# Block sums, bonus sums and transposes of an RWKV-7 inverse issued one step later than the vector operations that they read

## The chip, the cores and the metric

The kernel runs on one core of a Trainium2 chip. Its five engines each work through their own instructions in order: TensorE (PE in the profile; PEld is its weight load), VectorE (DVE), ScalarE (ACT), GpSimd (POOL) and SyncE (SP). An instruction that waits for another engine holds up everything behind it on its own. The metric is the device time of one execution in microseconds; less is better.

## The reference

Three transformer blocks follow one another on 512 tokens of width 1024. Only the second matters here: a normalised input is projected, a part of the columns goes through an RWKV-7 recurrence of six heads of 64, a part through block attention ("moba"), a part through a gated MLP; the three are joined, projected and followed by a feed-forward part. The recurrence, cut to what the change touches:

```
kk = heads(k * k_k)
kk = kk / jnp.maximum(jnp.linalg.norm(kk, axis=-1, keepdims=True), 1e-12)
k = k * (1.0 + (a - 1.0) * k_a)
...
def step(state, inp):
    r_t, w_t, k_t, v_t, kk_t, a_t = inp
    sa = jnp.einsum('bhij,bhj->bhi', state, -kk_t)
    state = (state * w_t[:, :, None, :]
             + sa[..., :, None] * (kk_t * a_t)[:, :, None, :]
             + v_t[..., :, None] * k_t[:, :, None, :])
    return state, jnp.einsum('bhij,bhj->bhi', state, r_t)
...
_, y = lax.scan(step, s0, xs)
...
bonus = jnp.sum(rh * kh * r_k.astype(jnp.float32), axis=-1, keepdims=True) * vh
out = (y + bonus.reshape(B, S, D_RWKV)) * g.astype(jnp.float32)
```

## The kernel before

The 512 recurrence steps are not run one by one. Six heads make three pairs (0, 1, 2), since two heads of 64 fill 128 partitions, and the tokens are cut in chunks of 64. Inside a chunk the steps become a triangular system, so each pair has three generators:

- `rw_e(p)` prepares: gates, exponentials and products of the inputs, and the bonus. VectorE makes t1 = r * r_k * k (line 1598), TensorE sums it over each head with a matrix of ones (`bon`, line 494 as all matmuls of the helper `mm`), VectorE multiplies the sum by v (line 1605). GpSimd makes two products, `b * kk` (line 1595) and `be` (line 1630; its tile shows as aa); VectorE's `ke` follows it (line 1631).
- `rw_solve(p)` inverts the triangular matrices. It makes the scores `sc` (masked on VectorE, line 1657), takes their diagonal 16 by 16 blocks, and spreads them over free columns in four products `mv` (line 1678; two on VectorE, two on GpSimd, 480, 352, 224 and 96 columns). TensorE sums each within blocks (`ab`), ScalarE copies the sum back (line 1683). Fifteen steps of two VectorE instructions (`tm`, `tc`, lines 1690 and 1692) give the inverse of the small blocks; it is spread into two matrices T (line 1695, one half on VectorE, one on GpSimd), transposed on TensorE (`Tn`, line 1700), and two levels of products (`inv`, `invT`, `invN`) with predicated copies (lines 1722 and 1723) extend it to 64 by 64.
- `rw_chain(p)` uses the inverse: `nat` transposes and their copies RW (lines 1844 to 1849), `akv`, W (copied on VectorE, line 1878), Rt, Y and the matrices M (masked to MN on VectorE, line 1900). Then the state goes through eight chunks: S on TensorE, st on VectorE (line 1914), one after the other.

What sets the order of instructions is a list of such Python generators that are stepped in turn. Each `yield` names a number of nanoseconds, and `run` always steps the generator whose sum of yields is smallest. These numbers are a schedule on paper, not times. Three calls of `run` hold the work of this part, each beside a share of the attention (`mo`, the moba generator: `at` scores, their softmax on VectorE and ScalarE with the exponentials `prob`, `pT` transposes, `ao`):

```
run(par.rest(), mo.part(MOP[0]))
run(slow(CS, rw_chain(0)), rw_solve(1), rw_e(2), mo.part(MOP[1]))
run(slow(CS, rw_chain(1)), rw_solve(2), mo.part(MOP[2]), rw_end(0))
```

The names used below: **stage A** is the end of the projections (`pj`) with `rw_solve(0)` and `rw_e(1)`, up to 1632 us in the profile; **stage B** is the second of these lines, to 1702 us; **stage C** the third, to 1762 us. `lg`, `mean`, `hs` and `hb` belong to `rw_end`, the normalisation and gate of a finished pair. All matmul results take one of 8 PSUM banks.

Of the kernel before, what the change touches and what calls it, by code (L numbers as in the profile page):

```python
# [16 lines left out]
OP = mybir.AluOpType  # L17
# [297 lines left out]
def kernel(ctx: ExitStack, tc: tile.TileContext, A, out):  # L315
    nc = tc.nc
    V, P, SC, PE = nc.vector, nc.gpsimd, nc.scalar, nc.tensor
# [7 lines left out]
    def T(name, dt=F32, n=512):  # L325
        return heap.tile([128, n], dt, name=name, tag="t")
# [4 lines left out]
    def SM(name, n, dt=F32):  # L331
        assert n <= 32
        return glob.tile([128, n], dt, name=name, tag="sm", bufs=24)

    def PS(name="ps"):
        return psum.tile([128, 512], F32, name=name, tag="ps")
# [6 lines left out]
    def vec(n, i=0, w=1):  # L343
        o, _ = _VOFF[n]
        return vecs[:, o + i:o + i + w]

    def con(n, i=0, w=None):
        o, ww = _COFF[n]
        w = ww if w is None else w
        return cons[:, o + i:o + i + w]  # L350
# [13 lines left out]
    def tok(t):  # L364
        return slice(128 * t, 128 * t + 128)
# [127 lines left out]
    def mm(ps, a, b, start, stop, **kw):  # L493
        PE.matmul(ps, a, b, start=start, stop=stop, **kw)  # L494
# [82 lines left out]
    def nosync(a, b):  # L577
        tc.add_manual_dep(a.ins, b.ins.name,
                          mybir.DependencyInfo(mybir.DependencyClass.NoSync, mybir.DependencyReason.DATA),
                          reason="table")  # L580
# [9 lines left out]
    def act(out_, in_, func, **kw):  # L590
        o = SC.activation(out_, in_, func, **kw)
        nosync(o, phase["mark"])
        phase["ops"].append(o)
# [157 lines left out]
    for k in range(KD):  # L751
# [4 lines left out]
        h, l = hx(k)  # L756
# [101 lines left out]
    for o in range(0, _NM, 512):  # L858
        a = T("mf")
        w = min(512, _NM - o)  # L860
# [446 lines left out]
    for e in range(NE):  # L1307
# [29 lines left out]
        for q in range(8):  # L1337
            w, rel = ws.raw()
            for kk in range(2):
                f = 2 * q + kk  # L1340
                p, c, j = f // 8, (f // 4) % 2, f % 4
# [239 lines left out]
    bon = {}  # L1581
    el = {}

    def rw_e(p):

        rT, kT, vT = ya.pop(p), ya.pop(3 + p), ya.pop(6 + p)
        kkn, b, l = kk.pop(p), aa.pop(p), lw.pop(p)
        cum = T("cum")
        V.tensor_tensor_scan(cum, r64, l, 0.0, op0=OP.mult, op1=OP.add)
        yield 800  # L1590

        t1 = T("t1")
        V.tensor_scalar(t1, b, -1.0, vec("rwkv_k_a_2", p), op0=OP.add, op1=OP.mult)
        V.scalar_tensor_tensor(kT, t1, 1.0, kT, op0=OP.add, op1=OP.mult)
        P.tensor_tensor(b, b, kkn, op=OP.mult)
        yield 1200

        V.scalar_tensor_tensor(t1, rT, vec("rwkv_r_k_2", p), kT, op0=OP.mult, op1=OP.mult)
        pb = PS("bon")
        mm(pb, con("blk64"), t1, True, True)  # L1600
        at = l
        V.tensor_tensor(at, cum, l, op=OP.subtract)
        yield 1500
        bon[p] = t1
        V.tensor_tensor(t1, pb, vT, op=OP.mult)
        c8 = cum.rearrange("p (n c) -> p n c", c=64)
        ke = T("ke")
        V.tensor_tensor(ke.rearrange("p (n c) -> p n c", c=64), c8[:, :, 63:64].to_broadcast([128, 8, 64]), c8,
                        op=OP.subtract)
        yield 1500  # L1610
        pc = SM("pc", 8)
        act(pc, c8[:, :, 63], AF.Exp)
        ei = T("ei")
        act(ei, cum, AF.Exp, scale=-1.0)
        act(at, at, AF.Exp)
        yield 1400
        act(cum, cum, AF.Exp)
        act(ke, ke, AF.Exp)
        V.scalar_tensor_tensor(at, kkn, -1.0, at, op0=OP.mult, op1=OP.mult)
        yield 1300  # L1620
        bh = kkn
        V.tensor_tensor(bh, b, ei, op=OP.mult)
        yield 800
        V.tensor_tensor(cum, cum, rT, op=OP.mult)
        yield 800
        kh = ei
        V.tensor_tensor(kh, kT, ei, op=OP.mult)
        yield 800
        be = b
        P.tensor_tensor(be, b, ke, op=OP.mult)  # L1630
        V.tensor_tensor(ke, kT, ke, op=OP.mult)
        yield 1400
        el[p] = at, cum, bh, kh, be, ke, vT, pc

# [2 lines left out]
    def rw_solve(p):  # L1637
# [10 lines left out]
        for t in range(TT):  # L1648
# [6 lines left out]
            for h in range(2):  # L1655
                a = sb[h][:, 512 * t:512 * t + 512]
                V.tensor_tensor(a.rearrange("p (x s) -> p x s", x=2), pss[h].rearrange("p (x s) -> p x s", x=2), m4,
                                op=OP.mult)
# [11 lines left out]
        i32, i16 = c32.rearrange("p (x i) -> p x i", x=8), c16.rearrange("p (x i) -> p x i", x=8)  # L1670
        V.tensor_scalar(i16, i32[:, :, :16], con("half32", 0, 1), None, op0=OP.mult)
        V.scalar_tensor_tensor(i16, i32[:, :, 16:], con("half32", 1, 1), i16, op0=OP.mult, op1=OP.add)

        ab = []
        for g in range(4):
            w = 15 - 4 * g
            mv = T("mv")
            (P if g % 2 else V).tensor_tensor(mv[:, :32 * w].rearrange("p (j x i) -> p j x i", j=4, x=8),
                               i16[:, None, :, 4 * g + 1:].to_broadcast([128, 4, 8, w]),
                               con("eye16", 4 * g, 4)[:, :, None, None].to_broadcast([128, 4, 8, w]), op=OP.mult)  # L1680
            ps = PS("ab")
            mm(ps[:, :32 * w], con("blk16"), mv[:, :32 * w], True, True)
            SC.copy(mv[:, :32 * w], ps[:, :32 * w])
            ab.append(mv[:, :32 * w].rearrange("p (j x i) -> p j x i", j=4, x=8))
            yield 700
        t16, m16 = tc.rearrange("p (x i) -> p x i", x=8), tm.rearrange("p (x i) -> p x i", x=8)
        P.tensor_copy(t16, con("eye16")[:, None, :].to_broadcast([128, 8, 16]))
        for j in range(15):
            w = 15 - j
            V.tensor_tensor(m16[:, :, :w], ab[j // 4][:, j % 4, :, j % 4:], t16[:, :, j:j + 1].to_broadcast([128, 8, w]),  # L1690
                            op=OP.mult)
            V.tensor_tensor(t16[:, :, j + 1:], t16[:, :, j + 1:], m16[:, :, :w], op=OP.add)
            yield 500
        for h in range(2):
            (P if h else V).tensor_tensor(
                Tt[h].rearrange("p (x b i) -> p x b i", x=4, b=8), t16[:, 4 * h:4 * h + 4, None, :].to_broadcast([128, 4, 8, 16]),
                con("own16")[:, None, :, None].to_broadcast([128, 4, 8, 16]), op=OP.mult)
            pa = PS("Tn")
            for t in range(TT):
                PE.transpose(pa[:, tok(t)], Tt[h][:, tok(t)], ident)  # L1700
            SC.copy(Tn[h], pa)
            yield 800
# [34 lines left out]
    def e0():  # L1737
        while "exp" not in flag:
            yield 1000
        yield from rw_e(0)  # L1740
        yield from bundle(rw_solve(0), wait(5000, rw_e(1)))
# [205 lines left out]
    mo = Persist(moba())  # L1947
# [3 lines that stand above are left out]
    m2 = lambda k, s=slice(0, 512): (m2p[k][0][:, s], m2p[k][1][:, s])  # L1951

# [513 lines left out]
```

## Time and profile before

| what | value |
|---|---|
| three runs, median (lowest to highest) | 3088.91 us (3085.46 to 3089.7) |
| the profiled execution | 3089.25 us |
| its span, first to last instruction | 3087.5 us |
| mean granted TensorE clock over the span | 0.973 |
| busy over the span: TensorE, VectorE, ScalarE, GpSimd | 92%, 41%, 26%, 15% |
| the three stages | 1590 to 1762 us of the span |

The shares of busy time are means over the whole program, most of which is large matrix products with TensorE full. The part that is changed covers some 172 of 3087.5 us and has to be read by itself. Times in the rows are microseconds from the span's start; a bracket after an instruction gives the idle time of its engine just before it and the instruction that ended that. A row with x4 stands for four instructions back to back. The granted clock is that of TensorE as a share of full speed.

### The profile page before, as it was taken

The numbers are of one execution on the slowest core, as the hardware profiler recorded it, in microseconds if no ns is written. First come the engines' busy times: TensorE is split into PE (matmuls) and PEld (weight loads), VectorE is DVE, ScalarE is ACT, GpSimd is POOL, SyncE is SP. The second block draws the span as 40 slices with busy tenths as digits, with TensorE's granted clock in tenths as the row PEclk, the third lists the DMA queues.
The fourth block names the chain that finished last, engine by engine and source line by source line (L and its number), as shares of the span: only waits on it lengthen the run. The fifth ranks groups of instructions, "written<-read, shape, count | busy, mean of one in ns | idle before, by whom it ended". The sixth has DMA issues, their size and how long they took to land.

```text
span 3087.5 us, 34890 instructions
## 1 busy us (share of the span) xinstructions
PE 2825.3 (92%) x13860; PEld 1847.5 (60%) x13860; DVE 1278.5 (41%) x2361; ACT 788.3 (26%) x1629; POOL 472.6 (15%) x440
## 2 busy tenths in 40 slices
PE   7989979998888888887997899999998989999999
PEld 4866564442222222224875678888886756788887
DVE  4157551112112111114376663333699753453334
ACT  3233220100000000004232332323343343442322
POOL 2035230000000000002220111001154332310100
PEclk8999979999999999998998999999999999999999
DMA  6123538999999999995110122323322212422221
GB/s 261 69 82 130 219 142 329 389 421 422 421 421 421 421 421 421 421 420 227 68 42 1 56 99 93 116 70 107 109 103 90 84 47 92 160 83 103 109 87 64
DMA packets 99011, 605.28 MB, mean 196 GB/s; under 512 B 11008, under 2 KB 11136, under 8 KB 31008
## 3 DMA queue, kind: packets, MB, share of 16 engines
q1 hardware_dynamic: 98640, 602.39, 49.6%
q8 instruction: 109, 1.79, 0.2%
q0 software_dynamic: 208, 0.66, 0.1%
q14 instruction: 54, 0.44, 0.0%
HBM read 592.52 MB, written 10.49 MB: 195 GB/s over the span
## 4 chain that ended last, share of the span: by engine, by line
PE 60%; DMA 24%; DVE 10%; ACT 2%; issue 2%; POOL 2%; SPq 0%; DVEq 0%; POOLq 0%; ACTq 0%
PE pj L494 25%; PE pn L494 15%; DMA wb<-in_w_up_dram 9%; DMA w<-in_w_up_dram 5%; DMA w<-in_w_down_dram 4%; PE pg L494 4%; DMA wb<-in_w_down_dram 4%; DVE cv L2146 2%; PE py L494 2%; PE at L494 2%; PE sp L494 1%; PE xs L494 1%; PE pc L494 1%; PE ao L494 1%; PE kv L494 1%
## 5 line engine op out<-in xcount | busy, mean ns | idle before, releaser
L443 DVE TENSOR_TENSOR wl<-w,wh 128x512 fp32r<-128x512 f32 (+1 forms) x422 | 299.0, 752 | 204.3 <-ACT wh L442 156.1
L494 PE MATMUL pg<-wb,xs 128*64 128x512 f32 x1184 | 284.7, 609 | 38.2 <-DMA wb<-in_w_up_dram 21.2
L442 ACT CAST wh<-w 128x512 fp32r<-128x512 f32 (+1 forms) x516 | 292.0, 617 | 99.1 <-PE pn L494 92.3
L494 PE MATMUL pg<-w,xs 128*64 128x512 f32 x824 | 197.0, 602 | 27.8 <-DMA w<-in_w_up_dram 15.0
L572 POOL TENSOR_TENSOR r<-m,mhalf 128x1 f32<-128x1 f32 x46 | 31.1, 678 | 1206.5 <-DVE m L618 1201.0
L494 PEld LDWEIGHTS pg<-wb,xs 128*64 128x64 f32 x1184 | 76.9, 138 | 220.8 <-issue 127.9
L494 PE MATMUL pn<-wh,fh 128*128 128x512 f32 x432 | 168.1, 389 | 0.0
L494 PE MATMUL pn<-wh,fl 128*128 128x512 f32 x432 | 168.1, 389 | 0.0
L494 PE MATMUL pn<-wl,fh 128*128 128x512 f32 x432 | 168.1, 389 | 0.0
L2146 DVE SCALAR_TENSOR_TENSOR cv<-glua,vecs,cv 128x507 f32<-128x507 f32 (+27 forms) x232 | 164.4, 735 | 4.2
L494 PE MATMUL py<-wb,hidT 128*64 128x512 f32 x600 | 142.4, 601 | 25.3 <-DMA wb<-in_w_down_dram 25.3
L443 POOL TENSOR_TENSOR wl<-w,wh 128x512 fp32r<-128x512 f32 x94 | 125.2, 1351 | 150.4 <-ACT wh L442 135.6
L494 PEld LDWEIGHTS pg<-w,xs 128*64 128x64 f32 x824 | 52.4, 136 | 152.6 <-issue 84.5
L494 PE MATMUL pj<-h2fh,wh 128*128 128x512 f32 (+1 forms) x376 | 141.4, 378 | 2.5 <-ACT h2fh L644 2.5
L494 PE MATMUL pj<-h2fl,wh 128*128 128x512 f32 (+1 forms) x376 | 141.7, 377 | 0.0
L494 PE MATMUL pj<-h2fh,wl 128*128 128x512 f32 (+1 forms) x376 | 141.6, 377 | 0.0
L1335 DVE TENSOR_TENSOR sg<-sg,pg 128x512 f32<-128x512 f32 x16 | 11.0, 688 | 292.1 <-PE pg L494 292.1
L494 PE MATMUL pj<-h3h,wh 128*128 128x512 f32 (+1 forms) x336 | 128.4, 382 | 0.6 <-ACT h3h L644 0.6
L494 PE MATMUL pj<-h3l,wh 128*128 128x512 f32 (+1 forms) x336 | 125.5, 373 | 0.6 <-DVE h3l L646 0.6
L494 PE MATMUL pj<-h3h,wl 128*128 128x512 f32 (+1 forms) x336 | 125.6, 374 | 0.0
L1352 DVE SCALAR_TENSOR_TENSOR yg<-py,gsl,g2h 128x512 f32<-128x512 f32 x16 | 12.0, 751 | 269.7 <-PE py L494 269.7
L494 PE MATMUL py<-w,hidT 128*64 128x512 f32 x424 | 102.4, 606 | 19.9 <-DMA w<-in_w_down_dram 19.9
(615 smaller groups left out, 5682.3 us busy)
## 6 DMA issues: line engine op xcount, KB each, us to landing
wb<-in_w_gate_dram SPq DMA_DIRECT2D x75, 1024.0 KB, 19.8
wb<-in_w_down_dram SPq DMA_DIRECT2D x75, 1024.0 KB, 19.8
wb<-in_w_up_dram SPq DMA_DIRECT2D x73, 1024.0 KB, 19.8
w<-in_w_down_dram SPq DMA_DIRECT2D x53, 1024.0 KB, 19.8
w<-in_w_up_dram SPq DMA_DIRECT2D x52, 1024.0 KB, 19.8
w<-in_w_gate_dram SPq DMA_DIRECT2D x51, 1024.0 KB, 19.8
w<-in_w_in_dram SPq DMA_DIRECT2D x35, 1024.0 KB, 4.9
w<-in_w_ff_dram SPq DMA_DIRECT2D x30, 1024.0 KB, 4.8
```

The costliest lines, as they stand in the source:

```text
L442: SC.copy(hi, src)
L443: (eng or V).tensor_tensor(lo, src, hi.bitcast(F32), op=OP.subtract)
L494: PE.matmul(ps, a, b, start=start, stop=stop, **kw)
L572: P.tensor_tensor(y, m, mhalf[:, :n], op=OP.pow)
L1335: V.tensor_tensor(sg, sg, pu, op=OP.mult)
L1352: V.scalar_tensor_tensor(a, py, gsl[:, e:e + 1], g2h, op0=OP.mult, op1=OP.mult)
L2146: V.scalar_tensor_tensor(acc[:, sh:], a[:, :512 - sh], w[j], acc[:, sh:], op0=OP.mult, op1=OP.add)
```

## The change

Three places are edited. In `rw_e` the bonus sum moves from right behind t1 to behind the exponentials, two yields later, and the product with v to the end. In `rw_solve` each block sum and its copy come one g later, behind the next product `mv`, with one more yield ahead of the last. And both T products come first, then a yield of 1500, then the transposes of both halves. The added yields are 700 + 1500 on paper for each pair.

```diff
--- before.py
+++ after.py
@@ -1596,13 +1596,9 @@
         yield 1200
 
         V.scalar_tensor_tensor(t1, rT, vec("rwkv_r_k_2", p), kT, op0=OP.mult, op1=OP.mult)
-        pb = PS("bon")
-        mm(pb, con("blk64"), t1, True, True)
         at = l
         V.tensor_tensor(at, cum, l, op=OP.subtract)
         yield 1500
-        bon[p] = t1
-        V.tensor_tensor(t1, pb, vT, op=OP.mult)
         c8 = cum.rearrange("p (n c) -> p n c", c=64)
         ke = T("ke")
         V.tensor_tensor(ke.rearrange("p (n c) -> p n c", c=64), c8[:, :, 63:64].to_broadcast([128, 8, 64]), c8,
@@ -1616,6 +1612,8 @@
         yield 1400
         act(cum, cum, AF.Exp)
         act(ke, ke, AF.Exp)
+        pb = PS("bon")
+        mm(pb, con("blk64"), t1, True, True)
         V.scalar_tensor_tensor(at, kkn, -1.0, at, op0=OP.mult, op1=OP.mult)
         yield 1300
         bh = kkn
@@ -1629,6 +1627,8 @@
         be = b
         P.tensor_tensor(be, b, ke, op=OP.mult)
         V.tensor_tensor(ke, kT, ke, op=OP.mult)
+        bon[p] = t1
+        V.tensor_tensor(t1, pb, vT, op=OP.mult)
         yield 1400
         el[p] = at, cum, bh, kh, be, ke, vT, pc
 
@@ -1671,18 +1671,27 @@
         V.tensor_scalar(i16, i32[:, :, :16], con("half32", 0, 1), None, op0=OP.mult)
         V.scalar_tensor_tensor(i16, i32[:, :, 16:], con("half32", 1, 1), i16, op0=OP.mult, op1=OP.add)
 
-        ab = []
-        for g in range(4):
-            w = 15 - 4 * g
-            mv = T("mv")
-            (P if g % 2 else V).tensor_tensor(mv[:, :32 * w].rearrange("p (j x i) -> p j x i", j=4, x=8),
-                               i16[:, None, :, 4 * g + 1:].to_broadcast([128, 4, 8, w]),
-                               con("eye16", 4 * g, 4)[:, :, None, None].to_broadcast([128, 4, 8, w]), op=OP.mult)
+        ab, mvs = [], []
+
+        def ab_sum(g):
+            w, mv = 15 - 4 * g, mvs[g]
             ps = PS("ab")
             mm(ps[:, :32 * w], con("blk16"), mv[:, :32 * w], True, True)
             SC.copy(mv[:, :32 * w], ps[:, :32 * w])
             ab.append(mv[:, :32 * w].rearrange("p (j x i) -> p j x i", j=4, x=8))
+
+        for g in range(4):
+            w = 15 - 4 * g
+            mv = T("mv")
+            mvs.append(mv)
+            (P if g % 2 else V).tensor_tensor(mv[:, :32 * w].rearrange("p (j x i) -> p j x i", j=4, x=8),
+                               i16[:, None, :, 4 * g + 1:].to_broadcast([128, 4, 8, w]),
+                               con("eye16", 4 * g, 4)[:, :, None, None].to_broadcast([128, 4, 8, w]), op=OP.mult)
             yield 700
+            if g:
+                ab_sum(g - 1)
+        yield 700
+        ab_sum(3)
         t16, m16 = tc.rearrange("p (x i) -> p x i", x=8), tm.rearrange("p (x i) -> p x i", x=8)
         P.tensor_copy(t16, con("eye16")[:, None, :].to_broadcast([128, 8, 16]))
         for j in range(15):
@@ -1695,6 +1704,8 @@
             (P if h else V).tensor_tensor(
                 Tt[h].rearrange("p (x b i) -> p x b i", x=4, b=8), t16[:, 4 * h:4 * h + 4, None, :].to_broadcast([128, 4, 8, 16]),
                 con("own16")[:, None, :, None].to_broadcast([128, 4, 8, 16]), op=OP.mult)
+        yield 1500
+        for h in range(2):
             pa = PS("Tn")
             for t in range(TT):
                 PE.transpose(pa[:, tok(t)], Tt[h][:, tok(t)], ident)
```

The number of instructions is the same on every engine, and the order of GpSimd and SyncE does not change. TensorE, VectorE and ScalarE differ from the first bonus sum (about 1568 us in the profile) to the last `invT` of pair 2 (1761 us); ahead of it and behind it all orders are the same.

TensorE in stage B, from the last `pT` of pair 0's attention step (bon is the bonus sum of pair 2, akv and nat are pair 0's chain). Before:

```order
L1791 MATMUL pT<-cons,prob 128x128 x3
L494 MATMUL bon<-t_9078,cons 128x512
L494 MATMUL akv<-RW,sc_8623 128x128
L494 MATMUL akv<-RW,sc_8624 128x128
L1844 MATMUL nat<-cons,lwd 128x128
L1844 MATMUL nat<-cons,aa 128x128
L1844 MATMUL nat<-cons,ke 128x128
L1844 MATMUL nat<-cons,ya_8013 128x128
L494 MATMUL ao<-probT,v_8466 64x512 x2
```

and now:

```order
L1802 MATMUL pT<-cons,prob 128x128 x3
L494 MATMUL akv<-RW,sc_8623 128x128
L494 MATMUL akv<-RW,sc_8624 128x128
L1855 MATMUL nat<-cons,lwd 128x128
L1855 MATMUL nat<-cons,aa 128x128
L1855 MATMUL nat<-cons,ke 128x128
L1855 MATMUL nat<-cons,ya_8013 128x128
L494 MATMUL ao<-probT,v_8466 64x512 x2
```

The bonus sum has left this place; it now stands 34 rows further down, behind the first M group and an ao. The first block sums of pair 1, with W, Y, akv, Rt and M of pair 0's chain, before:

```order
L494 MATMUL ab<-mv,cons 128x480
L494 MATMUL W<-RW,T 128x128 x2
L494 MATMUL ab<-mv,cons 128x352
L494 MATMUL at<-qk 128x128 x2
L494 MATMUL Y<-sc_8623,W 64x128
L494 MATMUL Y<-sc_8624,W 64x128
L494 MATMUL Y<-sc_8623,RW 64x128
L494 MATMUL Y<-sc_8624,RW 64x128
L494 MATMUL ab<-mv,cons 128x224
L494 MATMUL akv<-RW,sc_8623 128x128
L494 MATMUL akv<-RW,sc_8624 128x128
L494 MATMUL Rt<-sc_8623,W 64x128
```

and now:

```order
L494 MATMUL W<-RW,T 128x128 x2
L494 MATMUL at<-qk 128x128 x2
L494 MATMUL Y<-sc_8623,RW 64x128
L494 MATMUL Y<-sc_8624,RW 64x128
L494 MATMUL ab<-mv,cons 128x480
L494 MATMUL akv<-RW,sc_8623 128x128
L494 MATMUL akv<-RW,sc_8624 128x128
L494 MATMUL Rt<-sc_8623,W 64x128
L494 MATMUL Y<-sc_8623,W 64x128
L494 MATMUL Rt<-sc_8624,W 64x128
L494 MATMUL Y<-sc_8624,W 64x128
```

W, the at of 128 columns and a pair of Y now stand ahead of the first block sum (480 columns), and akv, Rt and Y directly behind it; the other three block sums come after the M group. The transposes of pair 1 in the same stage, with the state chain (S, Y) of pair 0, before:

```order
L494 MATMUL M<-RW,bkz 128x128
L494 MATMUL Y<-rt,MN 128x64
L1700 MATMUL Tn<-cons,T 128x128 x8
L494 MATMUL S<-MN 128x128
L494 MATMUL inv<-T,sc_9047 128x128 x4
L494 MATMUL inv<-T,sc_9048 128x128 x4
L494 MATMUL S<-st,MN 128x128
L494 MATMUL Y<-rt,st 128x64
L1791 MATMUL pT<-cons,prob 128x128 x8
```

and now:

```order
L494 MATMUL M<-RW,bkz 128x128
L494 MATMUL S<-MN 128x128
L494 MATMUL Y<-rt,MN 128x64
L1711 MATMUL Tn<-cons,T 128x128 x4
L494 MATMUL S<-st,MN 128x128
L494 MATMUL Y<-rt,st 128x64
L1802 MATMUL pT<-cons,prob 128x128 x4
L1711 MATMUL Tn<-cons,T 128x128 x4
L1802 MATMUL pT<-cons,prob 128x128 x4
L494 MATMUL inv<-T,sc_9047 128x128 x4
```

One S moves ahead of the transposes, another with its Y goes between their halves, and eight of the attention's pT now stand ahead of the first inv. In stage C the first block sum of pair 2 stood ahead of W, lg and the at of 512 columns, and now stands behind them.

## Rows read from the trace of the kernel before

**Rows 1.** Stretches: length, each engine's busy us, TensorE clock, DMA share, GB/s.
```profile
1590.00:1612.00 22.00, 18.72 (x67) 13.31 (x67) 18.59 (x48) 6.23 (x14) 8.40 (x10) 0.84 0.00 1
...
1632.00:1656.00 24.00, 14.85 (x104) 9.45 (x102) 15.72 (x31) 6.49 (x19) 4.43 (x7) 0.85 0.00 1
...
1656.00:1683.00 27.00, 18.98 (x112) 13.35 (x112) 20.23 (x90) 7.39 (x24) 2.06 (x4) 0.88 0.00 1
...
1683.00:1702.00 19.00, 18.95 (x144) 16.95 (x145) 6.97 (x16) 5.12 (x10) 0.81 (x1) 0.91 0.00 1
...
1718.00:1746.00 28.00, 22.48 (x136) 14.63 (x137) 22.24 (x74) 9.09 (x25) 4.22 (x5) 0.88 0.24 81
```

**Rows 2.** TensorE's waits from 1590 to 1770: total, times, longest.
```profile
PE ab L494 <- DVE mv L1678: 10.2, 3, 5.3
PE bon L494 <- DVE t L1598: 5.9, 2, 4.2
```

**Rows 3.** The chain of waits from 1635 to 1658: start, us, what.
```profile
1636.36 2.05 PE bon L494 x2
...
1651.29 1.72 POOL aa L1630
...
1656.34 1.94 PE ab L494 x2
```

**Rows 4.** TensorE, stage B: start, us, instruction, [idle before, and releaser].
```profile
1631.59 0.55 PE L1791 MATMUL pT<-cons,prob 128*128 128x128 f32 x3
1636.36 2.05 PE L494 MATMUL bon<-t,cons 128*128 128x512 f32 x2 [4.22 <-DVE t L1598]
1638.20 1.06 PE L494 MATMUL akv<-RW,sc 128*128 128x128 f32 x4
...
1656.34 1.94 PE L494 MATMUL ab<-mv,cons 128*128 128x480 f32 x2 [5.27 <-DVE mv L1678]
```

**Rows 5.** ScalarE, stage B, the copy that makes akv's operand.
```profile
1628.38 0.27 ACT L1849 COPY RW<-nat 128x128 f32<-128x128 f32 x1
```

**Rows 6.** VectorE, stage B.
```profile
1638.44 0.69 DVE L1605 TENSOR_TENSOR t<-bon,ya 128x512 f32<-128x512 f32 x1 [1.63 <-PE bon L494]
...
1643.18 1.29 DVE L1657 TENSOR_TENSOR sc<-sc,cons 128x512 f32<-128x512 f32 x2 [3.60 <-PE sc L494]
...
1655.54 0.66 DVE L1678 TENSOR_TENSOR mv<-c,cons 128x480 f32<-128x480 f32 x1
...
1659.17 0.42 DVE L1878 COPY W<-W 128x256 f32<-128x256 f32 x1 [2.98 <-PE W L494]
...
1682.21 0.69 DVE L1695 TENSOR_TENSOR T<-tc,cons 128x512 f32<-128x512 f32 x1
```

**Rows 7.** TensorE, stage A.
```profile
1593.02 1.12 PE L494 MATMUL bon<-t,cons 128*128 128x512 f32 x2 [1.67 <-DVE t L1598]
1595.39 3.86 PE L494 MATMUL ab<-mv,cons 128*128 128x480 f32 x6 [1.25 <-DVE mv L1678]
```

**Rows 8.** TensorE, stage C.
```profile
1721.95 1.94 PE L494 MATMUL ab<-mv,cons 128*128 128x480 f32 x2 [3.63 <-DVE mv L1678]
1723.68 1.06 PE L494 MATMUL W<-RW,T 128*128 128x128 f32 x4
```

**Rows 9.** VectorE, stage C.
```profile
1724.78 0.42 DVE L1878 COPY W<-W 128x256 f32<-128x256 f32 x1 [2.13 <-PE W L494]
...
1728.03 0.30 DVE L1758 TENSOR_TENSOR at<-at,cons 128x128 f32<-128x128 f32 x1 [0.79 <-PE at L494]
```

**Rows 10.** VectorE, the state chain, stage B.
```profile
1685.45 0.29 DVE L1914 TENSOR_TENSOR st<-S,MN 128x128 f32<-128x128 f32 x1 [2.55 <-PE S L494]
```

**Rows 11.** VectorE's line 1594 in A and B, and GpSimd beside the latter.
```profile
1591.49 0.69 DVE L1594 SCALAR_TENSOR_TENSOR ya<-t,ya 128x512 f32<-128x512 f32 x1
...
1632.85 1.50 DVE L1594 SCALAR_TENSOR_TENSOR ya<-t,ya 128x512 f32<-128x512 f32 x1
...
1632.55 1.26 POOL L1595 TENSOR_TENSOR aa<-aa,kk 128x512 f32<-128x512 f32 x1 [19.98 <-DVE t L1593]
```

## The prediction

> **What bounds the kernel now.** I started from the table of stretches [rows 1]. The five stretches shown are the ones whose instruction order changes, in stages A (1590 to 1612 us), B (1632 to 1702) and C (1718 to 1746). The reader is to see that no engine is full in four of them: TensorE works 14.85 of 24 us in the second, VectorE 15.72. TensorE's mean granted clock is 0.84 to 0.88 there, so part of each runs at the lower of its two levels (1.2 instead of 2.4 GHz). DMA is idle but for 0.24 in the last. So this part is bound by hand-overs between engines. Only 1683 to 1702 is full: TensorE 18.95 of 19.
>
> The waits of TensorE [rows 2] then name what ends last. Block sums wait 10.2 us for the `mv` products, bonus sums 5.9 us for t1. Both are operands that VectorE or GpSimd makes, and the consumer stands directly behind in program order. The chain of waits [rows 3] shows that these are on the path: it goes through the bonus sum at 1636.36, through GpSimd's `be` at 1651.29 and through the block sum at 1656.34. A microsecond taken off here should reach the end, since what follows is the same order of instructions on every engine and no transfer fills those stages.
>
> **The change, part by part.** Nothing is added or removed; the sum consists of waits.
>
> *The bonus sum (edit a), stage B.* The bonus sum of pair 2 stands at the head of TensorE's queue from the last pT (1631.59 + 0.55 = 1632.14) to 1636.36 and costs a wait of 4.22 us; it then takes 2.05 us [rows 4]. The same pair of matmuls took 1.12 us in stage A [rows 7], so after the wait the engine was at the lower clock. Behind it stood `akv`, whose operand ScalarE had finished by 1628.38 + 0.27 [rows 5]: it was ready and not served for nine microseconds. With the sum moved behind the first `M` group, `akv` can start at about 1632.2 instead of 1638.20, 6.0 us earlier. How much of that gets through VectorE decides. VectorE has two waits there that come from the late TensorE, 1.63 us for the bonus sum and 3.60 us for the scores [rows 6]; both go, 5.2 us. Its product with vT, 0.69 us [rows 6], also moves behind the solve's first `mv` product. So that product, at 1655.54 now, comes 5.2 + 0.7 = 5.9 us earlier. The bounds are 4 us (TensorE's wait alone) and 8.3 us (all idle time of VectorE in that stretch, 24 - 15.72 [rows 1]). I take 5.9, because both waits have their cause directly in the moved instruction; the later wait of `ke` for GpSimd's `be` stays.
>
> *The block sums (edit b), stage B.* Before, ab of 480 columns waits 5.27 us [rows 4] with W, the third `at` group and Y behind it, and VectorE's copy of W waits 2.98 us in consequence [rows 6]. Afterwards W, at and Y are ahead of it. The 2.98 us can go entirely, or not at all if VectorE only reaches the recurrence when the sum and its copy are ready; between 0 and 3.0 I take 2.1, nearer the row, since some of the block sum's own wait remains (about 2.5 us, with a shorter queue behind it). Some VectorE work that stood inside the fifteen steps now runs ahead of them, which shortens the steps by what it lengthens the start: nothing. T of stage B, at 1682.21 now [rows 6], so comes 5.9 + 2.1 = 8.0 us earlier, with bounds 4 and 10.
>
> *The transposes (edit c).* Both T products go out first, and pair 1's first transposes now stand behind one S and Y of the state chain. An S step's answer took VectorE a wait of 2.55 us [rows 10], so the loss is up to that. Against it, 1683 to 1702 ran at 0.91 [rows 1]: 9% of 19 us, 1.7 us, can come back. I take zero; bounds +2.5 and -1.7.
>
> *Stage A.* The bonus sum of pair 1 leaves the place ahead of the first block sum. Its wait of 1.67 us goes, but the block sum, which waited 1.25 us more [rows 7], needs the same `mv` product at the same time. The wait becomes one of about 4 us, and what stands behind it starts no earlier. Zero; bounds: a gain of 2 us (a transpose wait covered by `at` work) and a loss of 2 us (lower clock behind the longer wait; the block sums ran at it before too, six taking 3.86 us [rows 7]).
>
> *Stage C.* Here W, lg and the last `at` group pass the first block sum. TensorE had waited 3.63 us there and then ran W at the lower clock in 1.06 us [rows 8]; VectorE waited 2.13 us for W and 0.79 us for at [rows 9]. They fit into TensorE's wait, so 2.9 us of VectorE's waits go. The stretch's clock of 0.88 over 28 us [rows 1] holds another 3.4 us, of which I count a third, because other waits remain. Gain 4.0 us, bounds 2 (transposes now behind the last pT and ao work) and 6.3.
>
> Sum: 0 - 8.0 + 0 - 4.0 = -12.0 us. The profiled execution took 3089.25 us (span 3087.5 and 1.75 around it), 0.34 above the median of the three runs, so 3089.25 - 12 gives **3077 us**.
>
> **Where a rule speaks against it.** `be` of stage B is a GpSimd product of two SBUF operands, and the edit brings VectorE's two-operand work closer around it. Beside a GpSimd product of this kind, VectorE's 128x512 instruction at 1632.85 took 1.50 us, and 0.69 us where none ran [rows 11]. GpSimd's product ended at 1632.55 + 1.26 = 1633.81, and VectorE's 0.54 us later, nearly its whole own duration. The Trainium skill, page "SBUF — State Buffer", section "Who interferes with whom", says that a VectorE instruction with two SBUF inputs and a GpSimd instruction that reads SBUF exclude each other, the later one waiting to the end of the first. This pair of rows agrees with it.
>
> **The rivals.**
> 1. *The stall only moves.* If VectorE is the real bound of stages B and C (20.23 of 27 us from 1656 to 1683 [rows 1]), the first `mv` product gains little, and only TensorE's 4.22 us wait is saved: 3089.25 - 4 = 3085 us. For it: the 10.2 us of block-sum waits are waits for VectorE or GpSimd. Against it: VectorE itself waits for TensorE in the same stretches (3.60, 2.98, 2.13).
> 2. *Slower: the state chain gets in front of the transposes.* In stages B and C the transposes come behind S and Y, which wait for VectorE's st. One such hop is 2.55 us [rows 10]; two in B and one in C would be 7.6 us, and the time 3089.25 + 7.6 = 3097 us, if T came no earlier. It decides from the point where T gains less than these hops cost. Against it: in B the state chain starts before T is ready, so its first hop is hidden when T is the later one.
> 3. *Exclusion by GpSimd.* If in each of the three stages one further VectorE instruction is held as above, for 0.8 us (1.50 - 0.69) up to `be`'s 1.72 us [rows 3], 2.4 to 5.2 us are lost from the 12: 3080 to 3082 us. For it: the 1.50 us row. Against it: `be` itself keeps its place in GpSimd's order and VectorE's `ke` waits for it anyway.
>
> **How the numbers follow.** Forecast 0.60; the stall only moves 0.18; slower 0.08; exclusion 0.14. The likeliest ends at 3077. Its bounds are -4 - 2 + 2.5 + 2 = -1.5 us with every term at its worst end and -10 - 6.3 - 1.7 - 2 = -20 at its best, which will not all fall together; half of each distance gives 3073 to 3082. Rival 3 lies in that, rival 1 at 3085 above it. For eight in ten the range goes from 3070 to 3085.5, which takes in rival 1's centre and leaves out the slower one. Differences under 0.2% (6.2 us) can't be told from none: faster than 3082.7 has 0.60 + 0.14 = 0.74, same 0.18, slower 0.08.
>
> **What would show it.** Edit a is right if `akv` of stage B starts about 1632 and no bonus sum waits over 1 us. It is wrong if `akv` is early and the first `mv` product still comes after 1653. Edit b: the first block sum of B at about 1650 with a wait near 2.5 us, that of C with a wait under 1.5 us, and VectorE's waits of 2.98 and 2.13 us gone. In A the first block sum should wait about 4 us and still start near 1595.4. T of B should stand at about 1674, and that of C some 12 us earlier than now. Edit c is right if from T to pair 1's last invT takes no longer than now (1682 to 1702). The forecast falls if T of B comes less than 4 us earlier, if the transposes wait for S, or if a stage after 1762 gives the gain back.

## The result and the profile after

The changed kernel takes 3063.86 us (median of 4, 3061.51 to 3067.9), against 3087.2 us for the kernel before (4 runs beside it, 3085.46 to 3089.7): a ratio of 0.9924, 95% interval [0.9912, 0.9936]. That is faster, and by 23 us instead of the 12 us forecast; the time lies below the range of 3070 to 3085.5. Its profiled execution took 3067.9 us with a span of 3066.1.

The first and last instruction of each stage tell where the time went. The line numbers of these rows are 9 to 11 higher than before. From the timelines of both kernels: the first `mv` product of a stage and T on VectorE, and the first `nat` transpose behind the last invT on TensorE, which ends the stage. Before (the products and T of stage B are in [rows 6]):

```profile
1594.59 0.66 DVE L1678 TENSOR_TENSOR mv<-c,cons 128x480 f32<-128x480 f32 x1
...
1610.96 0.69 DVE L1695 TENSOR_TENSOR T<-tc,cons 128x512 f32<-128x512 f32 x1
...
1627.52 0.27 PE L1844 MATMUL nat<-cons,lwd 128*128 128x128 f32 x1
...
1701.86 0.27 PE L1844 MATMUL nat<-cons,lwd 128*128 128x128 f32 x1
...
1721.14 0.66 DVE L1678 TENSOR_TENSOR mv<-c,cons 128x480 f32<-128x480 f32 x1
...
1744.76 0.69 DVE L1695 TENSOR_TENSOR T<-tc,cons 128x512 f32<-128x512 f32 x1
...
1761.43 0.27 PE L1844 MATMUL nat<-cons,lwd 128*128 128x128 f32 x1
```

After:

```profile
1594.11 0.66 DVE L1687 TENSOR_TENSOR mv<-c,cons 128x480 f32<-128x480 f32 x1
...
1609.40 0.69 DVE L1704 TENSOR_TENSOR T<-tc,cons 128x512 f32<-128x512 f32 x1
...
1624.27 0.27 PE L1855 MATMUL nat<-cons,lwd 128*128 128x128 f32 x1
...
1645.51 0.64 DVE L1687 TENSOR_TENSOR mv<-c,cons 128x480 f32<-128x480 f32 x1
...
1667.34 0.69 DVE L1704 TENSOR_TENSOR T<-tc,cons 128x512 f32<-128x512 f32 x1
...
1686.24 0.27 PE L1855 MATMUL nat<-cons,lwd 128*128 128x128 f32 x1
...
1705.63 0.64 DVE L1687 TENSOR_TENSOR mv<-c,cons 128x480 f32<-128x480 f32 x1
...
1725.18 0.69 DVE L1704 TENSOR_TENSOR T<-tc,cons 128x512 f32<-128x512 f32 x1
...
1738.72 0.27 PE L1855 MATMUL nat<-cons,lwd 128*128 128x128 f32 x1
```

Differences of these starts give the stretch that the change can touch: 1761.43 - 1594.59 = 166.84 us before, 144.61 us after, 22.2 us less. The rest of the program gave nothing of it back: from the last row to the end of the span it is 1326.07 us before and 1327.38 after. I use this stretch as the measure in all that follows, because it starts up to 8 us apart between profiled executions of the kernels below, which blurs a single time but not the stretch. A stretch is still that of one execution: the last section shows 1.5 us between executions with the same order.

| part | before | after | forecast | measured |
|---|---|---|---|---|
| A, `mv` product to T | 16.37 | 15.29 | 0 | -1.1 |
| A, T to the end | 16.56 | 14.87 | 0 | -1.7 |
| B, start to the `mv` product | 28.02 | 21.24 | -5.9 | -6.8 |
| B, product to T | 26.67 | 21.83 | -2.1 | -4.8 |
| B, T to the end | 19.65 | 18.90 | 0 | -0.75 |
| C, start to the `mv` product | 19.28 | 19.39 | 0 | +0.1 |
| C, product to T | 23.62 | 19.55 | -4.0 | -4.1 |
| C, T to the end | 16.67 | 13.54 | in the 4.0, as a loss | -3.1 |

Below, the part of a stage from T to its end is called its tail.

TensorE's rows after the change, which answer to [rows 4, 7, 8]: the block sums of A, B and C, and `akv` of B between the first two:

```profile
1594.82 1.97 PE L494 MATMUL ab<-mv,cons 128*128 128x480 f32 x2 [3.95 <-DVE mv L1687]
...
1628.72 0.61 PE L494 MATMUL akv<-RW,sc 128*128 128x128 f32 x4
...
1646.21 1.97 PE L494 MATMUL ab<-mv,cons 128*128 128x480 f32 x2 [3.05 <-DVE mv L1687]
...
1706.42 1.04 PE L494 MATMUL ab<-mv,cons 128*128 128x480 f32 x2 [1.35 <-DVE mv L1687]
```

`akv` follows the last pT without a wait, 4.45 us behind stage B's start instead of 10.7. The block sums still wait, 8.4 us in all (10.2 before): the waits of 3.95 and 3.05 us are the ones foreseen. Behind those two the block sum takes 1.97 us, in C, behind 1.35 us, 1.04.

### The profile page after: what moved, and what is told of

The parts are those of the page before. It is cut to its first block, busy times and chain, and to the rows that moved or that the text cites. A ratio compares the mean times of both kernels' runs of the same rounds, so it can differ in the third digit from the quotient of the medians.

```text
span 3066.1 us, 34893 instructions
## 1 busy us (share of the span) xinstructions
PE 2817.4 (92%) x13860; PEld 1845.3 (60%) x13860; DVE 1279.3 (42%) x2361; ACT 789.1 (26%) x1629; POOL 473.0 (15%) x440
## 4 chain that ended last, share of the span: by engine, by line
PE 61%; DMA 24%; DVE 10%; ACT 2%; issue 2%; POOL 2%; SPq 0%; POOLq 0%; DVEq 0%; ACTq 0%
PE pj L494 26%; PE pn L494 15%; DMA wb<-in_w_up_dram 9%; DMA w<-in_w_up_dram 5%; DMA wb<-in_w_down_dram 4%; PE pg L494 4%; DMA w<-in_w_down_dram 4%; DVE cv L2157 2%; PE py L494 2%; PE at L494 1%; PE sp L494 1%; PE xs L494 1%; PE pc L494 1%; PE ao L494 1%; PE kv L494 1%
## 5 line engine op out<-in xcount | busy, mean ns | idle before, releaser
L494 PEld LDWEIGHTS pg<-w,xs 128*64 128x64 f32 x824 | 52.5, 137 | 154.9 <-issue 84.9
## 6 DMA issues: line engine op xcount, KB each, us to landing
wb<-in_w_gate_dram SPq DMA_DIRECT2D x75, 1024.0 KB, 19.8
wb<-in_w_down_dram SPq DMA_DIRECT2D x75, 1024.0 KB, 19.8
wb<-in_w_up_dram SPq DMA_DIRECT2D x73, 1024.0 KB, 19.8
w<-in_w_down_dram SPq DMA_DIRECT2D x53, 1024.0 KB, 19.8
w<-in_w_up_dram SPq DMA_DIRECT2D x52, 1024.0 KB, 19.8
w<-in_w_gate_dram SPq DMA_DIRECT2D x51, 1024.0 KB, 19.8
```

## The experiments

Theory 1: the gain is a sum of hand-overs, each worth the wait that it no longer causes. Theory 2: it comes from the longer time of the solve on paper, which puts other work ahead of it. Theory 3, formed after the first runs: the paper time pays through the place of the chain's MN masks against the fifteen steps. The lag of an edit is the later place of an instruction in the text, its paper time the yields that it adds. All stretches are worked out as above. Kernels with an interval were timed several times beside the kernel before; the others are one time and a profile.

| kernel | time, us | ratio [95%] | stretch | A | B | C |
|---|---|---|---|---|---|---|
| before | 3087.2 | | 166.8 | 32.9 | 74.3 | 59.6 |
| changed | 3063.86 | 0.9924 [0.9912, 0.9936] | 144.6 | 30.2 | 62.0 | 52.5 |
| a only | 3081.02 | 0.998 [0.9971, 0.999] | 160.5 | 32.8 | 68.1 | 59.6 |
| b only | 3072.46 | 0.9958 [0.9941, 0.9975] | 152.7 | 31.4 | 68.0 | 53.3 |
| c only | 3082.61 | 0.9988 [0.9979, 0.9998] | 162.6 | 31.6 | 73.1 | 57.9 |
| without a | 3076.82 | one run | 153.0 | 30.2 | 70.3 | 52.5 |
| without b | 3081.33 | one run | 158.1 | 31.3 | 69.1 | 57.8 |
| without c | 3067.72 | one run | 148.7 | 33.1 | 62.4 | 53.3 |
| added yields only | 3080.67 | 0.9981 [0.9971, 0.999] | 157.2 | 29.1 | 72.1 | 56.0 |
| lag only | 3074.89 | 0.9955 [0.9938, 0.9972] | 153.9 | 33.2 | 66.1 | 54.6 |
| b's lag only | 3085.39 | one run | 161.2 | 33.4 | 73.2 | 54.6 |
| yields all at Tn | 3066.34 | one run | 145.7 | 31.3 | 62.3 | 52.1 |
| 4000 at Tn | 3069.6 | 0.9942 [0.9926, 0.9959] | 147.0 | 30.3 | 63.5 | 53.3 |
| 2000 at the steps | 3072.81 | one run | 156.6 | 35.7 | 66.3 | 54.6 |
| lag, chain 1.7 | 3071.24 | one run | 150.9 | 32.8 | 62.7 | 55.5 |
| filled wait | 3063.48 | one run | 144.3 | 29.6 | 62.2 | 52.5 |
| lag of two | 3071.93 | 0.995 [0.9937, 0.9964] | 151.2 | 31.5 | 64.9 | 54.9 |
| lag of two, 1400 | 3073.42 | one run | 150.8 | 32.0 | 64.8 | 53.9 |

For the kernels with an interval, the medians beside the kernel before and the stretches agree within 1.2 us but for two: the added yields gave 6.3 us by the medians and 9.6 by the stretch, 4000 at Tn 17.1 and 19.8. A fourth execution of 4000 at Tn took 9708.49 us, three times the others; nothing on record says why, and it is left out of the time above.

**One edit at a time.** The edit of each is that hunk of the diff alone on the kernel before.

> Edit a alone: only the two bonus sums and the products on them move, the order of all else is that of before. Theory 1 (a sum of hand-overs): the 4.22 us wait and its half-clock tail go, the first mv product of stage B comes 6 us earlier, the 15 steps of stage B keep their 20 us (1662.1 to 1682.2 before), so the time falls by 6 to 7 us, to about 3080 to 3082. Theory 2 (the gain comes from where the solve stands against the chain and the softmax, not from the bonus sum): the solve waits for its own operands anyway, at most 3 us are gained. Rival that the stall only moves: 1 to 4 us.

> Edit b alone (block sums one product later, one more yield of 700). Theory 1: the bonus sum's stall stays, W and the first at pass the block sum; VectorE's wait for W goes and the 15 steps of stage B shorten from 20 to about 14 us as in the changed kernel; 5 to 9 us less, 3078 to 3083. Theory 2: most of the steps' shortening needs the longer paper time of both edits b and c, so b alone gives under 4 us.

> Edit c alone (both T products, a yield of 1500, then both halves' transposes). Theory 1: it gains only in stage A (the invT wait of 1.7 us) and in the tail of stage C (from T to the last invT 16.7 us before, 13.6 after): 3 to 5 us less, 3083 to 3085. My recorded term: nothing, between 2.5 us more and 1.7 us less in stage B. Rival: the state chain ahead of the transposes costs 5 to 8 us.

a gave 6.3 us of the stretch, all in B, and left the steps at 20.2 us: theory 1. b gave 14.1, more than either theory said, with steps of 13.5 us, as theory 1 had them. c gave 4.2. The sum of the three, 24.6 us, is close to the 22.2 us of all together. The reverse, one edit undone in the changed kernel:

> Edits a and b without c (the transposes stay directly behind each T product). The stretch was 144.6 us with all three, 166.8 before. Edit c alone gave 4.2 us. Theory 1 (sum of parts): 147 to 149. Theory 3 (lag of b and its 700 do nearly all, c's 1500 adds only what stage A and the tail of C still have idle): 145 to 147.

> Edits b and c without a: the bonus sums back directly behind t1. Alone, a gave 6.3 us of the stretch, all of it in B. If the parts add: 144.6 + 6.3 = 151 us, B 68. If b and c already cover the bonus sum's stall: under 148.

> Edits a and c without b: block sums directly behind their products, no yield of 700. Sum of the parts alone: 166.8 - 6.3 - 4.2 = 156 us, against 144.6 with b. If b's place is only its paper time, c's 1500 would cover more of it: 150 or less.

Without a 8.3 us are lost, without b 13.5, without c 4.1: each part is within about 2 us of what it gave alone, so none of them hides behind another. Of the 4.1 us without c, 1.5 lie in B ahead of T, where the order is that of the changed kernel and only TensorE's clock was lower (last section); so whether c's part is theory 1's or the smaller one stays open.

**Lag and paper time.** Edits b and c move the issue and add a yield; edit a only moves it. These take the two apart: the yields alone on the kernel before, and the lag of all three, or of b, without them.

```diff
+        yield 700
         t16, m16 = tc.rearrange("p (x i) -> p x i", x=8), tm.rearrange("p (x i) -> p x i", x=8)
...
+            if h == 0:
+                yield 1500
             pa = PS("Tn")
```

> The kernel before with edit b's and c's added yields only (700 ahead of the 15 steps, 1500 ahead of the first transposes), nothing else moved in the text. Theory 1: nothing, within 3 us of before, since each consumer still stands right behind its producer. Theory 2: the longer paper time alone pushes the solve behind the chain's and the attention's work and gives 5 to 10 us.

> All three edits as written but without their added yields (700 and 1500), so the lag of the issue without the longer paper time. The measure is the stretch from the first mv product of stage A to the nat behind pair 2's last invT: 166.8 us before, 144.6 in the changed kernel, split A 32.9 and 30.2, B 74.3 and 62.0, C 59.6 and 52.5. Theory 1 (each consumer a step behind its producer is what pays): A 31, B 63 to 65, C 54, the whole within 4 us of the changed kernel. Theory 2 (the paper time pays): B above 67 and C above 56, the whole 152 or more.

> Edit b alone without its yield of 700. With that yield the stretch was 152.7 us (A 31.4, B 68.0, C 53.3). Theory 1: within 2 us of that. Theory 2: 157 or more, with the tail of C (T to the end 14.9 with the yield) back at 16.7.

The yields alone gave 9.6 us (6.3 by the medians) though each block sum and each bonus sum stays directly behind its product: theory 1 said nothing would come of them, and falls in that. The yields do put time on paper between the last copy and the steps and between T and its transposes, so they delay these consumers too. The lag alone gave 12.9 (11.8 by the medians), less than theory 1 asked for; the whole is above theory 2's 152 us, but B and C are below its 67 and 56. Neither theory holds by itself. The two add to 22.5 by the stretch and to 18.1 by the medians, where all together gave 23.3, so it is not shown that they simply add. For b, its lag gave 5.7 us and its 700 the other 8.4, with the tail of C back at 16.7 without it: theory 2.

**Where the paper time pays.** The first thought was VectorE's steps: in stage B the time from the first step to T is 20.1 us before and 13.5 after, with three of the chain's MN masks inside the steps before, and one after. Two kernels test that, one with the yields moved from the steps to the transposes, one with the masks moved by another means (the chain's factor 1.7 for 1.6, no yields).

```diff
-        yield 700
         ab_sum(3)
...
-        yield 1500
+        yield 2200
         for h in range(2):
             pa = PS("Tn")
```

> The changed kernel with its added paper time in one place: no yield of 700 ahead of the 15 steps, 2200 in place of 1500 ahead of the transposes; the sum is the same. Theory 3 (the 700 counts because it puts the chain's masks MN, which wait for TensorE, behind the steps): B's steps are back at 20 us, B at 64 to 66, the whole at 149 to 152. Rival (only the sum of the paper time counts): within 1 us of 144.6, steps at 13.5.

> The lag of all three edits without added yields, and instead the chain's factor on paper raised from 1.6 to 1.7, by which the last MN mask comes behind T in stages B and C without any delay of the solve. With the lag alone the stretch was 153.9 us, B's steps 20.2. Theory 3 (what pays is the place of the chain's masks against the steps, not the yields as such): steps of B 14 to 17 us, the whole 147 to 151. Rival (the yields help in another way): steps at 20, whole at 153 or more.

With all 2200 at the transposes the steps of B are back at 20.3 us, and the stretch is 145.7 in place of the 149 to 152 that theory 3 asked for: it falls there. What the steps lost, the part ahead of them had gained (2.8 us from the product to the first step, 8.3 in the changed kernel). The chain's factor gave a stretch of 150.9 us with steps of 16.1, which by itself is what theory 3 said; but that is 3.0 us of the 9.3 between the lag alone and the changed kernel, with 21.9 us from T to the end of B. What follows T is the place where most of it lies. The table of stretches from T to the end of A, B and C, first with the lag only:

```profile
1610.89:1628.14 17.25, 15.46 (x112) 12.43 (x111) 13.42 (x46) 8.11 (x23) 1.51 (x1) 1.00 0.00 1
1673.55:1694.26 20.71, 19.87 (x143) 17.88 (x144) 7.52 (x17) 5.12 (x10) 1.50 (x1) 0.84 0.00 1
1732.16:1748.83 16.67, 14.64 (x122) 13.57 (x123) 7.00 (x16) 4.27 (x8) 1.49 (x1) 1.00 0.37 136
```

and with all the paper time at the transposes:

```profile
1609.23:1624.52 15.29, 15.04 (x112) 12.26 (x111) 12.59 (x46) 8.19 (x23) 1.50 (x1) 1.00 0.00 1
1668.89:1686.84 17.95, 17.49 (x140) 15.26 (x141) 7.72 (x16) 5.12 (x10) 1.51 (x1) 1.00 0.00 1
1725.58:1738.91 13.33, 13.33 (x116) 12.72 (x116) 6.61 (x13) 4.01 (x7) 1.49 (x1) 1.00 0.41 146
```

The three together are 54.6 and 46.6 us: 8.1 of the 8.2 us between these two kernels. The first column after the length is TensorE's busy time with its matmuls in brackets, the last but two its clock. Each tail gains in its own way. A has 112 matmuls in both, and its idle time goes from 1.8 to 0.25 us. C is full in the second and has six matmuls fewer, which ran ahead of T. In B the clock goes from 0.84 to 1.00, with 143 and 140 matmuls. TensorE's timeline at the transposes of B, with the lag only:

```profile
1674.39 1.94 PE L1709 MATMUL Tn<-cons,T 128*128 128x128 f32 x8 [2.49 <-DVE T L1703]
1676.13 0.64 PE L494 MATMUL S<-MN 128*128 128x128 f32 x2
1676.56 3.60 PE L494 MATMUL inv<-T,sc 128*128 128x128 f32 x16
```

and with the paper time at the transposes:

```profile
1668.83 0.43 PE L494 MATMUL Y<-rt,st 128*128 128x64 f32 x2 [1.24 <-DVE st L1924]
1669.72 0.63 PE L1710 MATMUL Tn<-cons,T 128*128 128x128 f32 x4 [0.46 <-DVE T L1703]
1670.19 0.39 PE L494 MATMUL S<-st,MN 128*128 128x128 f32 x2
1670.41 0.60 PE L1801 MATMUL pT<-cons,prob 128*128 128x128 f32 x4
1670.85 0.60 PE L1710 MATMUL Tn<-cons,T 128*128 128x128 f32 x4
...
1671.72 1.06 PE L494 MATMUL inv<-T,sc 128*128 128x128 f32 x8
```

One wait of 2.49 us for T becomes two, 1.24 for the state and 0.46 for T. The eight transposes go from 1.94 to 1.23 us and the sixteen inv from 3.60 to twice 1.06: these run at the higher clock in the second kernel.

**How much paper time.** Two more sizes on the changed kernel: 4000 for 1500 at the transposes, and 2000 for 700 at the steps.

> The changed kernel with 4000 in place of 1500 ahead of the transposes: more of the attention and state chain goes ahead of them. If the gain of the tails is that work moved into the time in which TensorE waits for T, the tails (T to end: A 14.9, B 18.9, C 13.5) shorten by 1 to 2 us more at most, since TensorE is already full in them, and then get longer where T is ready and the transposes are not issued. Expected: B and C together 0 to 3 us longer than in the changed kernel, since nothing is idle there any more. Rival 2 as recorded (state chain ahead of the transposes costs a hop of 2.5 us each): 5 us longer or more.

> The changed kernel with 2000 in place of 700 ahead of the 15 steps. Theory 3: one MN mask is left inside B's steps; with more paper time more work goes ahead of them and the time from the mv product to the first step grows: B's start part 8.3 to 10 or 11 us, steps 12 to 13; in all 0 to 3 us longer than the changed kernel. Better than it only if the last mask leaves the steps without delaying the first.

4000 costs 2.4 us by the stretch, where rival 2 of the prediction asked for 5 or more; 1.5 of them lie in B ahead of T, where the order did not change. But by the times it costs 5.7 us (3069.6 against 3063.86, each timed beside the kernel before but not beside the other), so rival 2's price isn't ruled out at 4000. 2000 at the steps costs 12.0, four times what was expected: in A alone the time from product to T grows from 15.3 to 21.4 us. With the 700 kept, 1500 is the best of the sizes tried at the transposes (none, 1500, 4000); 2200 was tried only with the 700 taken away.

**The wait that is left.** TensorE still waits 8.4 us for `mv` products. One kernel fills the waits of A and B with matmuls on constants, into a PSUM bank that nobody reads. Another moves the 700 from the last block sum to the first, which puts twelve more pj ahead of it in A, and akv to M ahead in B and C; a third has 1400 there.

```diff
+            if g == 0 and p < 2:
+                pf = PS("fill")
+                for _ in range(6):
+                    mm(pf, con("blk16"), cons[:, :512], True, True)
             ps = PS("ab")
...
             if g:
+                if g == 1:
+                    yield 700
                 ab_sum(g - 1)
-        yield 700
         ab_sum(3)
```

> The changed kernel with six extra matmuls of 512 columns on constants ahead of the first block sum of pairs 0 and 1, into a PSUM bank that nobody reads: TensorE waits 3.95 and 3.05 us there. If the wait costs by itself and by the lower clock behind it, the filled wait keeps the clock up: the block sum takes 1.05 in place of 1.97 us and stages A and B are 1 to 2 us shorter each. If VectorE sets the pace there, nothing changes (within 0.5 us).

> The changed kernel with its 700 moved from the last block sum to the first one: the first block sum now stands one more group back (behind twelve more pj in A, behind akv and the M group in B and C), the paper time is the same. TensorE still waits 3.95, 3.05 and 1.35 us for the first mv product in the changed kernel, 8.4 us in all. If the lag is what pays before the steps, the waits go and the stretch falls from 144.6 to 138 to 142 us, the time to 3058 to 3061. If VectorE sets the pace there, as the fill experiment suggested for B, only A gains: 143 to 144 us, no difference that can be measured.

> The same with 1400 in place of 700 there, 700 more paper time in all. Within 2 us of the kernel with 700 if the sum of paper time is near its best; 3 us longer or more if the transposes now come too late, as with 4000 ahead of them (147.0 us).

The fill ran 5.3 us, over the end of the wait, so that in A the block sum came 1.0 us later behind its product than in the changed kernel. It then took 0.97 us in place of 1.97, and A was 0.55 us shorter; in B it came 1.8 us later and B was 0.24 longer. In all that is no difference, with the later sum and the higher clock not told apart. With the lag of two the wait for the products fell to 2.6 us, and the stretch became 6.6 us longer; 1400 did not change that (150.8). From TensorE's timeline of the kernel with 700, A and then B:

```profile
1591.07 1.64 PE L494 MATMUL ab<-mv,cons 128*128 128x480 f32 x4 [1.36 <-DVE mv L1687]
...
1606.40 0.63 PE L1712 MATMUL Tn<-cons,T 128*128 128x128 f32 x4 [2.20 <-DVE T L1705]
...
1644.08 0.45 PE L494 MATMUL Rt<-sc,W 128*64 128x128 f32 x4 [2.75 <-DVE W L1890]
...
1647.23 1.50 PE L494 MATMUL ab<-mv,cons 128*128 128x480 f32 x2
```

In A the time from product to T is 15.29 us, as in the changed kernel, with VectorE 14 us busy in both. TensorE, with its pj done early, waits 2.20 us at the transposes instead. In B the block sum starts 4.2 us behind its product, 0.7 in the changed kernel, and waits for nothing; but TensorE has waited 2.75 us for VectorE's W just ahead, nearly the 3.05 that went. The time to the first step is 0.7 us shorter there, and the loss of B comes behind it: 2.0 us in the steps and 1.5 in the tail. Whether the late sums or the missing 700 at the last of them cost this is not shown.

## Why the prediction was wrong

The direction was right, and so were the places where edits a and b act; the size was not, and one kind of gain was missing.

- *Edit a*: 5.9 us forecast, 6.8 measured in place in the full change and 6.3 of the stretch alone. `akv` came where it was expected. VectorE's waits for the bonus sum and the scores are both gone, 5.2 us. The other 0.7 was wrong: the product with v still stands ahead of the first `mv` product, at 1641.02. What came in its place is mainly the wait of 1.16 us of `ke` for GpSimd's `be`, which I had said would stay. Before, and then after the change:

```profile
1653.03 0.69 DVE L1631 TENSOR_TENSOR ke<-ya,ke 128x512 f32<-128x512 f32 x1 [1.16 <-POOL aa L1630]
```

```profile
1641.02 0.69 DVE L1631 TENSOR_TENSOR t<-bon,ya 128x512 f32<-128x512 f32 x1
...
1647.02 0.77 DVE L1629 TENSOR_TENSOR ke<-ya,ke 128x512 f32<-128x512 f32 x1
```

- *Edit b in B*: 2.1 us forecast, 4.8 measured. With the lag alone it was 2.5 (24.2 us from product to T), near the forecast. The other 2.3 came with the yields: the steps are 6.7 us shorter than with the lag alone and the time ahead of them 4.3 longer, where I had written that work moved out of the steps shortens them "by what it lengthens the start: nothing". Up to 1.5 of the 2.3 may be luck of this execution's clock (last section).
- *Stage C*: 4.0 us forecast up to T, 4.1 measured.
- *Stage A and the transposes*: the step that failed is "I take zero" for edit c, with stage A at zero and, in C, the transposes behind pT and ao as a loss. Together these parts gave 6.7 us (1.1 + 1.7 + 0.75 + 3.1).

I had priced the lag and not the yields. My sum of -12.0 us is what the lag alone measured (-12.9: A +0.3, B -8.2, C -5.0, against 0, -8.0 and -4.0 forecast). The added paper time I read only as a possible loss, the work that gets in front of the transposes. I did not ask where TensorE is idle around T. In B it waited 2.72 us at the end of VectorE's fifteen steps, and [rows 1] showed the sign of that in 1656 to 1683 (18.98 of 27 us busy). The tails of A and C stand in none of the rows that I read. The three tails, before and then after the change:

```profile
1610.96:1627.52 16.56, 14.47 (x106) 11.37 (x105) 13.42 (x46) 8.22 (x23) 1.51 (x1) 1.00 0.01 1
1682.21:1701.86 19.65, 18.82 (x143) 16.81 (x144) 7.52 (x17) 5.12 (x10) 1.50 (x1) 0.91 0.00 1
1744.76:1761.43 16.67, 14.79 (x123) 13.57 (x123) 7.00 (x16) 4.27 (x8) 1.50 (x1) 1.00 0.41 147
```

```profile
1609.40:1624.27 14.87, 14.45 (x110) 11.84 (x108) 12.82 (x46) 8.08 (x23) 1.51 (x1) 1.00 0.00 2
1667.34:1686.24 18.90, 18.90 (x146) 16.78 (x146) 9.05 (x20) 5.13 (x10) 1.51 (x1) 0.94 0.00 1
1725.18:1738.72 13.54, 13.52 (x117) 12.90 (x117) 6.62 (x13) 4.00 (x7) 1.49 (x1) 1.00 0.43 153
```

and the longest waits of TensorE there and just ahead of T before:

```profile
1625.37 2.32 PE L494 MATMUL invT<-T,X 128*128 128x128 f32 x16 [1.73 <-ACT X L1711]
...
1683.05 1.94 PE L1700 MATMUL Tn<-cons,T 128*128 128x128 f32 x8 [2.72 <-DVE T L1695]
...
1756.64 0.49 PE L494 MATMUL S<-st,MN 128*128 128x128 f32 x2 [1.20 <-DVE st L1914]
```

Of the 5.6 us that the tails lost, 4.4 were TensorE's idle time: 2.1 us to 0.4 in A, 0.8 to 0 in B, 1.9 to 0 in C. The waits of 1.73 us for X in A and of 1.20 us for the state in C are gone; the bound "a transpose wait covered by `at` work" named a gain of 2 us for A, and I took nothing of it. In C six matmuls ran ahead of T, among them the state chain's first S, and that is the rest. The tails of A and B hold more matmuls than before, not fewer. B's tail, which I had called full, was nearly so and gained only 0.75 us.

- *Rival 2* (the state chain in front of the transposes) named the right order and the wrong sign: S and Y did come ahead of them, and in the changed kernel the transposes of B wait neither for T nor for S. With all the paper time there one such hop shows, the 1.24 us for the state, and took the place of a longer wait for T. 4000 is a loss, of 2.4 us by the stretch and 5.7 by the times; TensorE waits for the state 1.03 us ahead of the transposes of B there and 0.57 us between those of C, less than the 2.55 for each hop that I had counted.
- *Rival 1* (the stall only moves) was wrong for the change. It is right for what remains: the lag of two took most of the block sums' wait away, a wait for W took its place in B, and nothing was gained.
- *Rival 3* (exclusion by GpSimd) shows once more in B and cost little. VectorE's line 1625 took 1.45 us where 0.69 is usual, beside GpSimd's `be`:

```profile
1641.62 1.45 DVE L1625 TENSOR_TENSOR ei<-ya,ei 128x512 f32<-128x512 f32 x1
...
1641.26 1.27 POOL L1628 TENSOR_TENSOR aa<-aa,ke 128x512 f32<-128x512 f32 x1 [2.90 <-DVE kk L1620]
```

The instruction ended at 1643.07, 0.54 us behind GpSimd's end at 1642.53, the same distance as in [rows 11]. That agrees with the rule of the Trainium skill, page "SBUF — State Buffer", section "Who interferes with whom", by which the later one waits to the end of the first.

- *The range* ended at 3070, 19 us below the profiled execution. I halved the distances to the bounds because they "will not all fall together". They did fall together: the 22.2 us of the stretch lie beyond the -20 of all good ends. Against the kernel with the lag alone, the paper time shortened all three stages (by 3.1, 4.1 and 2.1 us), so the gains had that cause in common, and the halving was not justified.

## What to carry to other kernels

When an edit delays a consumer in a schedule, price two things apart: the wait that it no longer causes, and the work that the longer paper time puts ahead of it. The second is read from the idle time of the engine on both sides of the consumer, in every stage, not only in the one that looks worst. Before taking a left-over wait away, look whether the engine waited for is itself idle: here moving the block sums once gained, and moving the first of them twice took a wait away and brought nothing.

## What was not expected of the hardware

Where the order is the same, a stage can repeat within 0.1 us: C took 59.57 us before and 59.63 with edit a alone, which leaves C as it was. The first `mv` product starts anywhere from 1588.79 to 1596.53 us in these executions.

But the clock can differ with the same order. From the first product to the first step of stage B, all engines do the same instructions in the same order in the changed kernel and in the one without c, and this took 8.29 and 9.83 us:

```profile
1645.51:1653.80 8.29, 7.59 (x40) 5.23 (x42) 5.87 (x22) 1.98 (x7) 2.40 (x3) 0.79 0.00 0
```

```profile
1645.53:1655.36 9.83, 9.13 (x40) 6.49 (x42) 5.86 (x21) 1.97 (x7) 2.40 (x3) 0.65 0.00 0
```

TensorE's clock was 0.79 in the first and 0.65 in the second. With 4000 at Tn it was again 9.83 us at 0.65. So differences of up to 1.5 us between two stretches can be the clock alone.

TensorE's clock after waits: the same two matmuls of 480 columns took 1.97 us behind waits of 3.95 and 3.05 us, 1.04 behind 1.35, and 0.97 behind matmuls that only filled the wait. The length of the wait does not decide it alone: with all yields at Tn they took 1.07 us behind 3.06,

```profile
1646.47 1.07 PE L494 MATMUL ab<-mv,cons 128*128 128x480 f32 x2 [3.06 <-DVE mv L1687]
...
1649.15 1.22 PE L494 MATMUL M<-bkz,W 128*128 128x256 f32 x2
```

and the lower clock came a little later instead: the two M of 256 columns took 1.22 us there and 0.70 in the changed kernel.
